# Moving the weight rings' slots in SBUF from 32 past a multiple of 64 bytes to a multiple of 64

## The chip, the cores and the metric

The kernel runs on one core of a Trainium2 chip. The metric is the device time of one execution in microseconds (us). Before the change it is 838.55 us, the median of 3 runs (837.41 to 838.63).

## The reference

A decoder trunk of two layers on one sequence of 256 tokens with 1,024 features, all in float32. Layer 0 is an S5 state-space mixer, layer 1 an attention with forget gates; each is followed by a mixture of 32 experts of which every token uses two. Cut to what matters here, the experts:

```python
for e in range(N_EXPERTS):                       # 32
    y = (jax.nn.silu(t @ w1[e]) * (t @ w3[e])) @ w2[e]   # w1, w3: 1024 x 256, w2: 256 x 1024
    out = out + gates[:, e:e + 1] * y
```

and around them

```python
h = h + gate * s5_mixer(modulate(rmsnorm(h), shift, scale))      # layer 0
h = h + gate * hier_moe(modulate(rmsnorm(h), shift, scale))
k, v, fcum = shared_kv(h)
h = h + gate * fox_mixer(modulate(rmsnorm(h), shift, scale))     # layer 1
h = h + gate * hier_moe(modulate(rmsnorm(h), shift, scale))
```

Each expert layer has 32 x 3 x 1 MB of weights. No weight is used twice, so every byte of them is read once from HBM: 297 MB in all, among them the matrices that make shift, scale and gate.

## The kernel before, in words

**Blocks and slots.** All large weights are laid out in HBM as blocks of 128 rows of 8,192 bytes (1 MB, [128, 2048] float32), one row for each SBUF partition. One DMA on SyncE's queue fetches a block into a slot, a tile named w (line 67, function fetch). The slots form a ring: new_slot (line 60) hands out the next one, and a block's DMA waits until the slot's last reader is through.

```python
 46  wpool = ctx.enter_context(tc.tile_pool(name="ring", bufs=ring))      # ring = 12
 65  def fetch(src):
 66      t = new_slot()
 67      nc.sync.dma_start(t, src)
 85      pool = es.enter_context(tc.tile_pool(name=name, bufs=n, side=side))   # in grow
```

**Rings that grow.** The 12 slots of the pool "ring" are always there. Where other tiles have been given back, grow (line 83) adds pools of slots: "ring2" (4 slots, line 337, from the experts of layer 0 on), "ring3" (5 slots, line 1072, during the experts of layer 0), "ring4" (3 slots, line 1364) and "ring5" (4 slots, line 1469) for the experts of layer 1. So layer 0's experts cycle through 21 slots, 5 of ring3 and then 16 others, and layer 1's through 19. ring3 is the only one on the right side of SBUF.

**Two sides.** Pools are placed one after the other, from the bottom of SBUF upwards (side left) or from its top downwards (side right), every tile at the next multiple of 32 bytes in its partition. On the left lie first the constants (pool "const": cols, line 96; h, line 98; and others), then the pool "small", then "ring", and above it what a stage needs. On the right are the tiles of the gating (uT, vg, uH, uL), ring3, the expert tiles P, Pr, a, aT, y, and most of the attention's tiles (xs, hn, oT, sgT, v, ws).

**The expert layers** (function moe, line 332 on). The experts go in 8 quads of 4. For a quad, gather (line 461, matmuls of line 470) collects up to 32 tokens for each of the four experts; first (line 499, matmuls of line 506) multiplies them by 8 blocks wa, the matrices w1 and w3; after silu and a transposition second (line 515, matmuls of line 521) multiplies by 4 blocks wb, the matrix w2; scatter (line 526, matmuls of line 528) adds the result to the tokens. load (line 326) issues the blocks ahead, in the order in which they are used (wa 8, wb 4, quad by quad), as far as slots are free. SyncE's queue is in order; it has 8 blocks under way and issues the next when one has landed.

**Other stages.** Before layer 0's experts runs the S5 loop (lines 796 to 1000), whose operations on VectorE (lines 840 to 951) work on tiles such as m1, m2 and cz above the ring. Between the two expert layers lie the shared keys and values and the attention (lines 1078 to 1470); there ScalarE and VectorE split each weight into two parts (lines 1125, 1126 into ws) and TensorE multiplies them (lines 1200, 1387, 1424).

Of the kernel before, what the change touches and what calls it, by code (L numbers as in the profile page):

```python
# [10 lines left out]
F32 = mybir.dt.float32  # L11
# [10 lines left out]
KD = 8  # L22
NE = 32
CAP = 32
NQ = NE // 4
EPS = 1e-6
BIG = 1e30
# [11 lines left out]
def trunk(ctx: ExitStack, tc: tile.TileContext, A, out, ring=12, ring2=4, ring3=5, ring4=3, ring5=4, lpb=2, TK=2):  # L39
# [3 lines left out]

    const = ctx.enter_context(tc.tile_pool(name="const", bufs=1))
    small = ctx.enter_context(tc.tile_pool(name="small", bufs=2))
    wpool = ctx.enter_context(tc.tile_pool(name="ring", bufs=ring))
    slots = [wpool] * ring
    turn_ = [0]
# [60 lines left out]
    V.memset(ones, 1.0)  # L109
    slot = const.tile([128, CAP], F32, name="slot")  # L110
    G.iota(slot, pattern=[[1, CAP]], base=1, channel_multiplier=0, allow_small_or_imprecise_dtypes=True)
    desc = const.tile([128, NE], F32, name="desc")
# [50 lines left out]
    def ada_cols_pe(name, j, put):  # L163

        ps = mm_tile()
        for b, w in enumerate([block(name, j, b) for b in range(4)]):
            for kk in range(2):
                for q in range(4):
                    PE.matmul(ps[32 * q:32 * q + 32, 0:256], sc32(2 * b + kk),
                              bands(w[:, 1024 * kk:1024 * kk + 1024])[:, q],  # L170
                              start=b + kk == 0, stop=b == 3 and kk == 1)
        put(ps)
        yield

    def ada_gate_pe(name, j, li, gbc, at_once=False):

        ps = mm_tile() if at_once else acc_tile()
        rows = small.tile([128, 512], F32, tag="rows", name="rows", bufs=1)
        G.memset(rows, 0.0)
        for n in range(2):  # L180
            nc.sync.dma_start(rows[32 * n:32 * n + 1, :], A["gbias"][li, n:n + 1, :])
        for b, w in enumerate([block(name, j, b) for b in range(4)]):
            for q in range(4):
                PE.matmul(ps[32 * q:32 * q + 32, :], sc32(2 * b + q // 2), w[:, 512 * q:512 * q + 512],
                          start=b == 0, stop=b == 3)
            if not at_once:
                yield
        ins = V.tensor_tensor(rows, ps, rows, op=OP.add)
        if not at_once:
            tc.keep_in_program_order(ins)  # L190
        yield
        for n in range(2):
            pt = mm_tile()
            PE.matmul(pt, pick[:, n:n + 1].to_broadcast([128, 128]), rows, start=True, stop=True)
            S.activation(gbc[:, 512 * n:512 * n + 512], pt, AF.Copy)
# [25 lines left out]
    def as_shift(bias, sh):  # L221
        return lambda ps: as_columns(ps, 8, sh, cols[:, bias:bias + 8])

    def as_gain(bias, lng, g):
        def put(ps):
            as_columns(ps, 8, g, cols[:, bias + 8:bias + 16])
            V.scalar_tensor_tensor(g, g, 1.0, cols[:, lng:lng + 8], op0=OP.add, op1=OP.mult)
        return put
# [80 lines left out]
    def router(l, sh, g):  # L309
# [12 lines left out]

    orders = [[(n, (l, q, j)) for q in range(NQ) for n, m in (("wa", 8), ("wb", 4)) for j in range(m)]
              for l in range(2)]
# [7 lines left out]
    def moe(l, sh, g, gbc, c36, slots_):  # L332
# [34 lines left out]
        def t2(n, w):  # L367
            return ma.tile([128, 2, w], F32, name=n)
# [78 lines left out]
        scs, xgs, Ps, acc = {}, {}, {}, []  # L447
        shp = [128, 4, CAP]

        def place(q):  # L450

            P = mb[0].tile([128, 2, 4, CAP], F32, tag="P", name="P", bufs=1)
            Pr = mb[0].tile([128, 2, 4, CAP], F32, tag="Pr", name="Pr", bufs=1)
            e = slice(4 * q, 4 * q + 4)
# [71 lines left out]
        def scatter(q, y, n, done=None):  # L526
            for i in range(2):
                PE.matmul(acc[i][n], scs[q][:, 128 * i:128 * i + 128], y[:, 512 * n:512 * n + 512],  # L528
                          start=q == 0, stop=q == NQ - 1, skip_group_check=True)
                if done:  # L530
                    done(i, n, acc[i][n])

        def overflow(rv):

            with tc.If(rv > CAP):
                gov = t2("gov", NE)
# [14 lines left out]
                gnext = t2("gnext", NE)  # L551
                with tc.For_i(0, NQ, 1) as q, tc.For_i(0, 2048, 512) as c:

# [61 lines left out]
        def experts(mosti, fill, done, tail=()):  # L615
            y = None
            for q in range(NQ):
                last = q == NQ - 1
                work = {}
                if q == NQ - 2:  # L620
                    scatter(q - 1, y, 1)
# [187 lines left out]
    for m in range(2):  # L809
# [5 lines left out]
    side = [ada_gate_pe("ada00g", 0, 0, gb00, True),  # L815
            ada_cols_pe("ada01", 0, as_shift(C_ADAB + 16, sh01)),
            ada_cols_pe("ada01", 1, as_gain(C_ADAB + 16, C_LNG + 8, g01)),
            ada_cols_pe("kvada", 0, as_shift(C_ADAB + 64, shkv)),
            ada_cols_pe("kvada", 1, as_gain(C_ADAB + 64, C_KVG, gkv))]
# [794 lines left out]
```

## Time and profile before

| | |
|---|---|
| median of 3 runs | 838.55 us (837.41 to 838.63) |
| the profiled execution | 838.87 us |
| its span, first to last instruction | 837.1 us |
| mean granted clock of TensorE | 0.932 |
| TensorE busy (matmuls) | 710.3 us, 85% |
| VectorE busy | 412.0 us, 49% |
| ScalarE busy | 218.8 us, 26% |
| DMA moved | 299.28 MB, mean 358 GB/s |
| of it the queue of the weights (q1) | 297.14 MB, 87.5% of 16 engines' span |

The span is what the trace covers; the time of an execution is 1.8 us more. A share of the DMA is the mean over the core's 16 DMA engines; each of them carries out rows (packets) one after the other, so that one may begin a little before the other's end and a full share reads 1.01. A block's time to landing runs from its issue on SyncE until all 128 rows are in.

### The profile page before, as it was taken

What the parts mean: (1) busy time and instruction counts of PE and PEld (TensorE: products, weight loads), DVE (VectorE), ACT (ScalarE), POOL (GpSimd) and SP (SyncE); (2) the same over time, 40 slices, a digit from 0 to 9 for tenths busy, and PEclk for the clock granted to TensorE, in tenths of its full rate; (3) what the DMA queues carried; (4) which work ended last, traced back from release to release, by engine and by line L of the source; (5) the groups of instructions that cost most, each with busy time, mean ns of one, the idle gap of its engine ahead of it and who ended that gap; (6) DMA issues with size and microseconds to landing.
All of it is one profiled execution on the core that took longest, in us unless ns stands there. A gap on an engine that the chain in (4) does not pass through costs nothing. (4 is left out here: it accounts for less than half of the span.)

```text
span 837.1 us, 13449 instructions
## 1 busy us (share of the span) xinstructions
PE 710.3 (85%) x5396; PEld 407.1 (49%) x5396; DVE 412.0 (49%) x1068; ACT 218.8 (26%) x498; POOL 51.8 (6%) x52
## 2 busy tenths in 40 slices
PE   3897999897899987676799988599998999887776
PEld 0674776584343333131286776488764333331311
DVE  7685999864422221120376589967654222221202
ACT  4332333252211110010234355456522111100100
POOL 2000000000000000000002106900000000000000
PEclk9998999998999999898769999789999999997887
DMA  9998956778999999999999996323879999999996
GB/s 370 418 417 346 385 175 254 302 300 324 418 419 420 419 418 420 420 417 416 421 418 377 412 380 230 128 104 105 350 313 404 418 420 419 419 420 419 417 413 251
DMA packets 41827, 299.28 MB, mean 358 GB/s; under 512 B 4632, under 2 KB 4760, under 8 KB 5664
## 3 DMA queue, kind: packets, MB, share of 16 engines
q1 hardware_dynamic: 41344, 297.14, 87.5%
q10 hardware_dynamic: 416, 1.23, 0.4%
q8 instruction: 44, 0.72, 0.3%
q14 instruction: 23, 0.19, 0.1%
HBM read 297.31 MB, written 1.05 MB: 356 GB/s over the span
## 5 line engine op out<-in xcount | busy, mean ns | idle before, releaser
L506 PE MATMUL mm<-w,xg 128*32 128x512 f32 x1024 | 144.3, 645 | 28.7 <-DMA w<-wa 10.9
L506 PEld LDWEIGHTS mm<-w,xg 128*32 128x32 f32 x1024 | 29.8, 112 | 118.2 <-issue 68.1
L478 ACT ACTIVATE xg<-mm,sh,g 128x128 f32<-128x128 f32 x64 | 29.3, 458 | 189.0 <-PE mm L470 172.8
L521 PE MATMUL mm<-w,aT 128*32 128x512 f32 x512 | 68.0, 647 | 12.5 <-DMA w<-wb 6.9
L1200 PE MATMUL acc<-ws,hn 128*128 128x512 f32 x288 | 74.2, 416 | 2.3 <-ACT hn L1164 2.3
L1126 DVE TENSOR_TENSOR ws<-w,ws 128x512 fp32r<-128x512 f32 x80 | 60.9, 765 | 29.6 <-ACT ws L1125 29.3
L470 PE MATMUL mm<-Pr,h 128*128 128x128 f32 x512 | 64.2, 279 | 11.2 <-DVE Pr L458 11.2
L470 PEld LDWEIGHTS mm<-Pr,h 128*128 128x128 f32 x512 | 59.8, 192 | 26.0 <-issue 18.6
L528 PE MATMUL acc<-y,Sc 128*128 128x512 f32 x128 | 65.8, 638 | 6.5 <-DVE y L524 6.5
L1125 ACT ACTIVATE ws<-w 128x512 fp32r<-128x512 f32 x80 | 50.1, 629 | 71.3 <-PE acc L1200 45.9
L1200 PEld LDWEIGHTS acc<-ws,hn 128*128 128x128 f32 x288 | 56.4, 199 | 18.1 <-ACT hn L1164 2.5
L476 DVE TENSOR_SCALAR xg<-mm,g,sh 128x128 f32<-128x128 f32 x64 | 26.2, 410 | 73.1 <-ACT xg L478 73.1
L524 DVE TENSOR_TENSOR y<-mm,gbc 128x512 f32<-128x512 f32 x32 | 22.1, 692 | 68.9 <-PE mm L521 68.6
L489 DVE COPY Sc<-mm 128x256 f32<-128x256 f32 x16 | 6.8, 425 | 86.6 <-PE mm L487 86.6
L511 ACT ACTIVATE a<-mm 128x256 f32<-128x256 f32 x16 | 6.1, 384 | 161.9 <-PE mm L506 161.9
L528 PEld LDWEIGHTS acc<-y,Sc 128*128 128x128 f32 x128 | 22.7, 198 | 47.0 <-issue 29.8
L512 DVE TENSOR_TENSOR a<-a,mm 128x256 f32<-128x256 f32 x16 | 6.7, 420 | 77.5 <-ACT a L511 77.5
L521 PEld LDWEIGHTS mm<-w,aT 128*32 128x32 f32 x512 | 14.1, 113 | 53.0 <-issue 37.1
L981 PE MATMUL acc<-w,uT 128*128 128x512 f32 x64 | 31.9, 645 | 5.7 <-ACT uT L970 5.7
L805 PE MATMUL mm<-hnT,w 128*64 128x128 f32 x512 | 32.4, 286 | 2.7 <-ACT hnT L275 2.7
L805 PEld LDWEIGHTS mm<-hnT,w 128*64 128x64 f32 x512 | 30.7, 140 | 4.4 <-ACT hnT L275 3.7
L1387 PE MATMUL acc<-hn,ws 128*128 128x256 f32 x192 | 28.5, 303 | 2.6 <-DVE ws L1126 2.6
(334 smaller groups left out, 980.9 us busy)
## 6 DMA issues: line engine op xcount, KB each, us to landing
w<-wa SPq DMA_DIRECT2D x128, 1024.0 KB, 19.9
w<-wb SPq DMA_DIRECT2D x64, 1024.0 KB, 19.9
w<-ada SPq DMA_DIRECT2D x36, 1024.0 KB, 10.6
w<-ada00s SPq DMA_DIRECT2D x8, 1024.0 KB, 18.0
w<-kvada SPq DMA_DIRECT2D x8, 1024.0 KB, 9.8
w<-win SPq DMA_DIRECT2D x4, 1024.0 KB
w<-ada00g SPq DMA_DIRECT2D x4, 1024.0 KB, 19.0
w<-woutv SPq DMA_DIRECT2D x4, 1024.0 KB, 17.6
```

Source lines behind the costliest of these rows:

```text
L470: PE.matmul(px[:, 128 * c4:128 * c4 + 128], h[:, i, 128 * c:128 * c + 128], Pr[:, i].rearrange("p a b -> p (a b)"), start=i == 0, stop=i == 1)
L476: V.tensor_scalar(xg[:, c], src, g[:, c:c + 1], sh[:, c:c + 1], op0=OP.mult, op1=OP.add)
L478: S.activation(xg[:, c], src, AF.Identity, bias=sh[:, c:c + 1], scale=g[:, c:c + 1])
L506: PE.matmul(ph[32 * s:32 * s + 32, :], xg[:, k, 32 * s:32 * s + 32], w[:, 512 * s:512 * s + 512], start=k == 0, stop=k == KD - 1)
L521: PE.matmul(py[32 * s:32 * s + 32, :], aT[:, 128 * f + 32 * s:128 * f + 32 * s + 32], w[:, 512 * s:512 * s + 512], start=f == 0, stop=f == 1)
L528: PE.matmul(acc[i][n], scs[q][:, 128 * i:128 * i + 128], y[:, 512 * n:512 * n + 512], start=q == 0, stop=q == NQ - 1, skip_group_check=True)
L805: PE.matmul(ps[64 * v:64 * v + 64, 128 * hh:128 * hh + 128], w[:, k, c0:c0 + 64], hnT[:, k, v::2], start=k == 0 and hh == 0, stop=k == KD ...
L981: PE.matmul(val[t][n], uT[:, m, 128 * t:128 * t + 128], wval[m // 2][:, c0:c0 + 512], start=m == 0, stop=m == 7)
L1125: S.activation(o[:, 0], w, AF.Copy)
L1126: V.tensor_tensor(o[:, 1], w, o[:, 0].bitcast(F32), op=OP.subtract)
L1200: PE.matmul(pk[i], src[:, k, a, 128 * i:128 * i + 128], w[:, b], start=k + a + b == 0, stop=k == KD - 1 and b == 1)
L1387: PE.matmul(po[:, 256 * m2:256 * m2 + 256], w[:, bb, kk, 128 * m2:128 * m2 + 128], hq[:, k, a, :], start=k + a + bb + m2 == 0, stop=k == K ...
```

## The change

Two tiles that nothing reads or writes are placed, one on each side: 224 bytes per partition on the left after the pool "small" and ahead of "ring", and 32 bytes on the right, at the very top.

```diff
@@ -22,6 +22,7 @@
 KD = 8
 NE = 32
 CAP = 32
+PAD_LEFT, PAD_RIGHT = 56, 8
 NQ = NE // 4
@@ -43,6 +44,9 @@
     const = ctx.enter_context(tc.tile_pool(name="const", bufs=1))
     small = ctx.enter_context(tc.tile_pool(name="small", bufs=2))
+
+    for i, (sd, n) in enumerate((("left", PAD_LEFT), ("right", PAD_RIGHT))):
+        ctx.enter_context(tc.tile_pool(name=f"pad{i}", bufs=1, side=sd)).tile([128, n], F32, name=f"pad{i}")
     wpool = ctx.enter_context(tc.tile_pool(name="ring", bufs=ring))
```

Everything placed later moves: on the left 224 bytes up, on the right 32 bytes down. Each address then changes its remainder by 64 from 32 to 0 or from 0 to 32; what lies ahead of the pads stays. The addresses in a partition, in bytes:

| tile | before | remainder by 64 (by 256) | after | remainder by 64 (by 256) |
|---|---|---|---|---|
| cols, rows of 1,424 bytes | 1,152 | 0 (128) | 1,152 | 0 (128) |
| h, rows of 4,096 bytes | 2,592 | 32 (32) | 2,592 | 32 (32) |
| slots of "ring", 12 | 23,328 + 8,192 k | 32 (32) | 23,552 + 8,192 k | 0 (0) |
| slots of ring2, ring4, ring5 | 121,632 or more | 32 (32) | 121,856 or more | 0 (0) |
| slots of ring3, 5 | 188,384 + 8,192 k | 32 (224) | 188,352 + 8,192 k | 0 (192) |
| cosT, sinT | 147,872 and 156,064 | 32 | 148,096 and 156,288 | 0 |
| m1, m2, cz (S5 loop) | 187,840 and others | 0 | 188,064 and others | 32 |
| uH, uL, vg, first ws | 184,288 and others | 32 | 184,256 and others | 0 |
| attention's ws | 217,056 and others | 32 | 217,024 and others | 0 |
| xs, hn, oT, sgT, xf, v | 184,256 and others | 0 | 184,224 and others | 32 |
| P, Pr, a, aT, y (experts) | 167,904 and others | 32 | 167,872 and others | 0 |

The program built from it has the same instructions on every engine and queue, in the same order and with the same waits; only addresses differ.

## Rows read from the trace of the kernel before

**Rows 1.** Windows: stretch; PE, PEld, DVE, ACT, POOL busy us (count); clock; DMA share; GB/s.
```profile
208.00:406.00 198.00, 162.44 (x1074) 61.81 (x1073) 43.80 (x123) 19.46 (x42) 0.22 (x2) 0.95 1.01 419
636.00:828.00 192.00, 160.18 (x1014) 60.06 (x1015) 40.81 (x110) 16.90 (x38) 0.00 (x0) 0.91 1.00 415
```

**Rows 2.** Waits of SyncE's queue, 205 to 415 us: us in total, times, longest.
```profile
SPq L67 <- DMA w<-wa: 91.8, 44, 3.5
SPq L67 <- DMA w<-wb: 53.9, 26, 2.1
...
SPq L67 <- PE mm L506: 6.8, 12, 3.4
```

**Rows 3.** Timeline of TensorE, last quad of layer 0: start, length, [idle time before].
```profile
388.00 1.06 PE L506 MATMUL mm<-w,xg 128*32 128x512 f32 x8 [1.32 <-SPq L535]
390.49 1.06 PE L506 MATMUL mm<-w,xg 128*32 128x512 f32 x8 [1.43 <-SPq L535]
...
395.48 1.93 PE L506 MATMUL mm<-w,xg 128*32 128x512 f32 x8 [0.57 <-SPq L535]
```

**Rows 4.** Chain of waits, its longest link: start, length in us.
```profile
811.28 7.34 DMA w<-wa
```

**Rows 5.** Windows: sum over 100 to 160 us, the S5 loop.
```profile
sum 60.00, PE 57.30 PEld 38.67 DVE 58.12 ACT 18.23 POOL 0.00; mean PE 19.10 PEld 12.89 DVE 19.37 ACT 6.08 POOL 0.00
```

**Rows 6.** DMA, 208 to 406 us: queue, packets, MB, share; issues, us to landing.
```profile
GB/s 407 424 424 415 420 419 422 417 414 422 424 422 417 415 422 419 417 417 422 417 422 419 420 419 419 414 422 422 424 412 417 415 424 420 409 422 424 420 401 422
...
q1 hardware_dynamic: 11353, 82.67, 100.8%
...
w<-wa SPq DMA_DIRECT2D x48, 1024.0 KB, 19.9
```

**Rows 7.** DMA, 636 to 827 us.
```profile
q1 hardware_dynamic: 10908, 79.40, 100.3%
```

**Rows 8.** DMA, 166.4 to 168.6 us: 2.2 us in which the weights come unhurried.
```profile
DMA packets 122, 0.93 MB, mean 425 GB/s; under 512 B 8, under 2 KB 8, under 8 KB 8
...
q1 hardware_dynamic: 122, 0.93, 100.3%
```

**Rows 9.** DMA, 8 to 9 us: q10 carries rows of h.
```profile
q10 hardware_dynamic: 33, 0.14, 32.8%
```

**Rows 10.** DMA, 3.8 to 4.8 us: q10 carries rows of cols.
```profile
q10 hardware_dynamic: 40, 0.06, 15.2%
```

**Rows 11.** Windows of 12.5 us in layer 0, columns as in rows 1.
```profile
232.20:244.70 12.50, 10.96 (x70) 4.55 (x70) 2.38 (x9) 0.38 (x1) 0.00 (x0) 1.00 1.01 420
244.70:257.20 12.50, 12.50 (x86) 4.96 (x85) 3.03 (x6) 1.83 (x4) 0.00 (x0) 1.00 1.01 417
...
297.40:309.90 12.50, 11.54 (x93) 5.65 (x91) 3.25 (x11) 2.21 (x5) 0.00 (x0) 1.00 1.01 417
284.90:297.40 12.50, 10.98 (x77) 3.67 (x77) 3.48 (x8) 1.30 (x3) 0.00 (x0) 1.00 1.01 419
```

**Rows 12.** Groups by line and shape, whole run: xcount | busy us, mean ns of one.
```profile
L1030 ACT ACTIVATE ws<-w 128x512 fp32r<-128x512 f32 x16 | 9.9, 628 | 6.7 <-PE mm L1053 4.5 <-DVE ws L1031 2.2
...
L1164 ACT ACTIVATE hn<-xf 128x512 fp32r<-128x512 f32 x8 | 4.8, 624 | 1.3 <-DVE xf L1160 1.2
...
L1031 DVE TENSOR_TENSOR ws<-w,ws 128x512 fp32r<-128x512 f32 x16 | 10.8, 688 | 4.0 <-ACT ws L1030 3.9
L951 DVE TENSOR_TENSOR m<-m,cosT 128x1024 f32<-128x1024 f32 x8 | 9.8, 1224 | 0.2
...
L1165 DVE TENSOR_TENSOR hn<-xf,hn 128x512 fp32r<-128x512 f32 x8 | 5.3, 690 | 0.6 <-ACT hn L1164 0.5
...
L719 DVE TENSOR_TENSOR sinT<-sinT,cosT 128x1024 f32<-128x1024 f32 x2 | 2.4, 1218 | 0.0
...
L1424 PE MATMUL acc<-ws,oT 128*128 128x512 f32 x96 | 25.0, 406 | 0.0
...
L1053 PE MATMUL mm<-ws,uH 128*128 128x512 f32 x64 | 20.8, 404 | 0.2 <-DVE ws L1031 0.2
```

## The prediction

> **What bounds the kernel now.** I read the windows first, since the page's busy shares mix stages. In two long stretches, 208 to 406 us and 636 to 828 us, the DMA engines are busy all the time (shares 1.01 and 1.00) and move 419 and 415 GB/s, while TensorE is busy for 162.4 of 198 and 160.2 of 192 us [rows 1]. These are the expert layers. The waits of SyncE's queue confirm who sets the pace there: of the 210 us from 205 to 415, the queue spends 91.8 + 53.9 = 145.7 us waiting for earlier weight blocks to land, and 6.8 us for TensorE to free a slot [rows 2]. The timeline of TensorE shows the same from the other side: in the last quad of layer 0 its groups of eight matmuls start at 388.00, 390.49, 392.98 and 395.48 us, so one block of 1 MB every 7.48 / 3 = 2.49 us, with up to 1.43 us of idle time before each group [rows 3]. The program ends the same way: the chain of waits begins with 7.34 us of a weight transfer [rows 4]. So in 390 of the 837.1 us the rate at which rows of 8,192 bytes are written into the ring slots is the time of the kernel. Elsewhere it isn't: in the S5 loop, from 100 to 160 us, VectorE is busy for 58.1 of 60 us [rows 5].
>
> **What the change does to that.** It issues nothing new. Every engine and queue keeps its instructions, their order and their waits; no DMA is added, split or moved. Only addresses move: ring slots go from 32 past a multiple of 64 to a multiple of 64. The whole question is therefore the price of a write, read or row at one offset against the other, at three kinds of places.
>
> **Term 1, the weight rows in the two stretches.** How many: queue q1 carries 82.67 MB in 198 us and 79.40 MB in 191 us [rows 6, 7]. Together 162.07 MB are 154.6 blocks of 1.0486 MB, or 19,784 rows of 8,192 bytes, 1,236 for each of the 16 DMA engines. One nanosecond per row is so worth 1.24 us of the kernel.
>
> What a row costs now: in a quiet window of 2.2 us, 122 packets on q1, 8 of them signals under 512 bytes, take 100.3% of 16 engines, which is 35.3 us, or 309 ns for each of the 114 rows (the signals are under 0.1 us in all) [rows 8]. The rows of h (4,096 bytes, also 32 past a multiple of 64) take 32.8% of 16 us for 33 packets: 159.0 ns [rows 9]. Two points give a line: 150 ns for 4,096 bytes, 0.0366 ns per byte, with 9.0 ns fixed per row.
>
> What an aligned row costs: the trace has one transfer with a destination that already is a multiple of 64, the table cols at byte 1,152, with rows of 1,424 bytes. Its 40 packets from 3.8 to 4.8 us take 15.2% of 16 us, 60.8 ns each [rows 10]. The line through the unaligned rows gives 0.0366 × 1,424 + 9.0 = 61.1 ns. The aligned row is 0.3 ns below it, within the rounding of the shares. I take 0.3 ns, because it is the only row in this trace at the new offset: 0.3 × 1.24 = **0.4 us saved**. The bounds: nothing at one end (61.1 and 60.8 are then the same), and at the other the whole fixed part of 9.0 ns, if alignment were all that it is made of: 11.1 us. A loss is not excluded by principle, but an aligned row has no more bytes than an unaligned one, and cols shows none.
>
> The nearest check on a finer address than 64 is inside this kernel. The right-hand ring has slots at 224 past a multiple of 256, the left-hand slots lie at 32 past it, and one round of the ring takes five blocks into the right and sixteen into the left. By count of blocks the right-hand ones fill 244.7 to 257.2 and 297.4 to 309.9 us: 417 and 417 GB/s, against 420 and 419 in the left-hand stretches just ahead [rows 11]. That is 0.6% for 192 bytes of offset, so for the 32 bytes of this change a sixth, 0.1% of 389 us, again 0.4 us.
>
> A rule of the Trainium skill speaks on just this. DMA: Bandwidth & Descriptors, section "How a descriptor splits into AXI transactions", says that a transaction must start at a multiple of 256 bytes, so that a row with another start pays for bytes that it doesn't use. By it a row would cost 257 beats of 32 bytes in a left-hand slot now and 263 in a right-hand one, 2.3% more; the windows show 0.6%, so the trace agrees in sign and not in size. By the rule the change takes one beat off each row.
>
> **Term 2, the engines' operands.** TensorE reads the slots, ScalarE and VectorE split them, and many tiles trade offsets (some lose the multiple of 64: those of the S5 loop, and hn, oT, xs in the attention part). Same work at both offsets is in the trace. ScalarE's copy of 512 columns takes 628 ns from and to tiles 32 off a multiple of 64, and 624 ns between aligned ones; VectorE's subtraction of 512 columns takes 688 ns 32 off and 690 ns aligned; with 1,024 columns 1,218 ns 32 off and 1,224 ns where the result is aligned; TensorE's 512-column matmul has a mean of 404 ns with uH (32 off) and 406 ns with oT (aligned) as weights [rows 12]. The differences between 32 off and aligned are -6 to +4 ns, of both signs. I take **0**. In the two stretches even 4 ns would be hidden behind the 1.43 us of idle time per block [rows 3].
>
> **Term 3, everything else.** The pads take 256 bytes of each partition and no instruction writes them: 0.
>
> **Sum.** The profiled execution took 838.87 us, span 837.1 and 1.8 around it; its 0.4 us less is 838.5. The median of the three runs is 838.55, 0.3 below the profiled one, and the prediction is for a median: 838.55 - 0.4 = **838.2 us**. What a measurement of this kernel can tell from no change is about 0.2%, 1.7 us, so this is "the same".
>
> **Rivals.**
> 1. *One piece less per row.* The write of a row is cut at some coarser grid, and the slots' start off that grid costs one more 32-byte piece. Price: 32 × 0.0366 = 1.17 ns per row, 1.45 us in all, 837.1 us. For: the right-hand slots are slower by 0.6%. Against: cols shows 0.3 and not 1.2 ns. It stays just under 1.7 us, so mostly "the same". The skill's section named above is this case.
> 2. *The offset costs only under load.* A row takes 309 ns when the queue is quiet; but in the two stretches a block takes 389 / 154.6 = 2.516 us, where 8 rows and a signal would take 8 × 309 + 9 = 2.481 us. Over 154.6 blocks that is 5.4 us of waiting which no quiet row shows. If writes that straddle 64 bytes are what waits (two neighbouring rows' pieces meeting in one place, say), most of it goes: 838.55 - 5.4 = 833.1 us. For: the loss exists, and the trace has no aligned transfer under full load. Against: it comes in part as single gaps, the rate of the forty slices between 208 and 406 us lies between 401 and 424 GB/s [rows 6], which looks like something that happens now and then and not to every row. If it and the fixed 9.0 ns both went, the time would be 822; nothing supports that.
> 3. *Slower: the S5 loop loses its alignment.* The tiles m1, m2, cz and their like go from a multiple of 64 to 32 past one, in the stretch from 100 to 160 us where VectorE is busy for 58.1 of 60 us [rows 5]. If VectorE's operations there grew by 5%, the kernel would take 2.9 us longer, 841.4. It decides from 1.7 / 58 = 2.9%, some 36 ns on a 1,224 ns operation. Against: 1,218 ns with both operands 32 off [rows 12].
> The change can't fail to do what it says: the addresses are fixed when the program is built.
>
> **How the numbers follow.** Forecast (0 to 1 us saved) 0.50, rival 1 0.14, rival 2 in whole or in part 0.27, rival 3 0.09. Rival 1 lies so near the limit that I give 0.04 of it to "faster". Faster by over 0.2%: 0.27 + 0.04 = 0.31. Within: 0.50 + 0.10 = 0.60. Slower: 0.09. The range reaches down to 832.0, so that all of rival 2 and 1.1 us of run to run differences are in it (the runs differ by 1.2 us), and up to 839.8, which leaves out rival 3 and half the tail above the median: about 0.15 outside. The forecast's own range is 837.3 to 839.2.
>
> **What would show it right or wrong.** Right: in the profile after, the windows of the two stretches again give 419 and 415 GB/s within 1, a block of layer 0's last quad every 2.49 us, 19.9 us from issue to landing [rows 6]. Rival 1 shows as 0.4% more: 2.48 us per block, 421 GB/s. Rival 2 as a rate of 422 GB/s or more and a landing of 19.6 us. Rival 3 as longer means of VectorE's lines 918 to 951 with the two stretches unchanged in length. I am wrong if the rate of the loaded stretches moves by over 1%, either way: then the cost of an offset under load is not that of a quiet row, and the step from cols to the weights is the one that failed.

## The result, and the profile after

The change brings **830.09 us** (median of 4 runs, 827.79 to 830.81) against 838.59 us (median of 4 runs of the kernel before, 837.41 to 840.59). The ratio is 0.9891, with a 95% interval from 0.9863 to 0.992: faster by 1.1%, where I had forecast 0.4 us and no difference that can be measured. The profiled execution took 830.81 us with a span of 829.0, where it was 838.87 and 837.1 before; the mean granted clock of TensorE is 0.938 (0.932 before).

The windows of the two expert layers come first, since the forecast hung on their rate. The columns are those of rows 1.

```profile
208.00:403.00 195.00, 162.42 (x1070) 61.66 (x1070) 43.65 (x123) 19.29 (x41) 0.22 (x2) 0.95 1.01 425
632.00:819.00 187.00, 156.87 (x1012) 59.84 (x1012) 40.49 (x110) 16.70 (x37) 0.00 (x0) 0.93 1.01 424
```

The DMA engines are as full as before (1.01), and move 425 and 424 GB/s where they moved 419 and 415 [rows 1]. TensorE has the same work in it (162.42 us against 162.44 in the first). The view of the DMA for the first of these windows gives the GB/s of forty slices, the queue of the weights and a block's time from issue to landing, as rows 6 do:

```profile
GB/s 418 429 429 420 429 427 427 423 425 427 430 422 425 430 427 423 423 430 427 422 425 425 430 427 425 425 429 425 427 429 418 418 429 429 425 425 427 427 410 429
...
q1 hardware_dynamic: 11367, 82.78, 100.8%
...
w<-wa SPq DMA_DIRECT2D x48, 1024.0 KB, 19.6
```

The queue carries 82.78 MB in 195 us, where it took 198 us for 82.67 [rows 6]. The slices have moved as a whole: from 401 to 424 they went to 410 to 430, so it isn't that a few gaps were closed. A block lands after 19.6 us (19.9 before).

The timeline of TensorE in the last quad of layer 0, as in rows 3:

```profile
385.75 1.06 PE L510 MATMUL mm<-w,xg 128*32 128x512 f32 x8 [1.26 <-SPq L539]
388.18 1.94 PE L510 MATMUL mm<-w,xg 128*32 128x512 f32 x8 [1.36 <-SPq L539]
...
393.04 1.89 PE L510 MATMUL mm<-w,xg 128*32 128x512 f32 x8 [0.50 <-SPq L539]
```

(The change adds four lines, so L506 is now L510 and L67 is L71.) Three blocks in 7.29 us are one in 2.43 us, against 2.49 [rows 3]. Still TensorE waits for each of these blocks, and the waits of SyncE's queue, 205 to 412 us, say the same as rows 2:

```profile
SPq L71 <- DMA w<-wa: 92.1, 46, 3.1
SPq L71 <- DMA w<-wb: 53.7, 27, 2.2
...
SPq L71 <- PE mm L510: 4.6, 10, 2.1
```

So the bound is what it was, weight rows on their way into the ring. It is the row that has become cheaper.

**Where the 8.1 us of the spans went.** The starts of the weight rows in the trace date each of the 282 blocks (from 0) of a profiled execution. Blocks 58 to 141 and 206 to 281 are those of the expert layers that wait for little but the DMA. Beside the pair stand means over two groups of kernels, one execution of each: before with the experiments e1, e2 and e4 below, whose left-hand slots are off a multiple of 256, and after with e3 and e6, whose left-hand slots are on one.

```
us                                      before   after   before, e1, e2, e4   after, e3, e6
start of the span to block 58           194.0    194.9   194.2                194.4
block 58 to 141, layer 0's last         209.0    205.7   208.6                205.7
block 141 to 206, in layer 1            232.4    230.1   230.5                229.7
block 206 to 281, the last              188.2    185.1   188.0                185.1
block 281 to the end                     13.6     13.2    13.5                 13.1
```

The two stretches of the expert layers give 3.3 and 3.1 us in the pair, 2.8 and 2.9 in the means. The kernel's first weight stream gets shorter too (the 24 blocks from block 3 to block 27 in 60.2 us, 61.4 before), but the S5 loop behind it takes what it took, and block 58 comes no sooner. The stretch between the layers differs by 2.3 us in the pair and 0.9 in the means, and by up to 3.2 us within the first group, so I count nothing there.

### The profile page after: what moved, and what is told of

It is laid out like the page before. It is cut to its first block, busy times and chain, and to the rows that moved or that the text cites. A ratio compares the mean times of both kernels' runs of the same rounds, so it can differ in the third digit from the quotient of the medians.

```text
span 829.0 us, 13449 instructions
## 1 busy us (share of the span) xinstructions
PE 707.3 (85%) x5396; PEld 409.8 (49%) x5396; DVE 411.8 (50%) x1068; ACT 218.7 (26%) x498; POOL 51.9 (6%) x52
## 5 line engine op out<-in xcount | busy, mean ns | idle before, releaser
L510 PE MATMUL mm<-w,xg 128*32 128x512 f32 x1024 | 141.7, 636 | 27.1 <-DMA w<-wa 11.8
L510 PEld LDWEIGHTS mm<-w,xg 128*32 128x32 f32 x1024 | 29.8, 112 | 115.8 <-issue 68.4
L532 PE MATMUL acc<-y,Sc 128*128 128x512 f32 x128 | 64.0, 623 | 7.0 <-DVE y L528 7.0
## 6 DMA issues: line engine op xcount, KB each, us to landing
w<-wb SPq DMA_DIRECT2D x64, 1024.0 KB, 19.6
```

The source lines that it names most:

```text
L510: PE.matmul(ph[32 * s:32 * s + 32, :], xg[:, k, 32 * s:32 * s + 32], w[:, 512 * s:512 * s + 512], start=k == 0, stop=k == KD - 1)
```

## The experiments

Open were: which pad does it, which remainder counts (64, as the slots' new place suggests, or something coarser), whether it is the DMA or an engine's operands, whether the read or the write, and why the quiet rows of the prediction showed nothing. The first five keep the kernel whole and only change the pads; the last four are nothing but a stream of blocks. Each stream is a single execution, and its stages are compared with one another.

**e1_both32: every ring slot on a multiple of 64, none on one of 256.**

```diff
-PAD_LEFT, PAD_RIGHT = 56, 8
+PAD_LEFT, PAD_RIGHT = 8, 8
```

> Pads of 32 and 32 bytes: left-hand slots at 64 past a multiple of 256, right-hand ones at 192 past, all at multiples of 64. Theory A (a row costs more under load when its slot starts off a multiple of 64, whatever the coarser remainder): a block every 2.453 us in the expert layers as with the change, time 830 us, within 2 of the changed kernel. Theory B (the grid is 256 bytes; only slots at its multiples gained): the left-hand slots are off the grid again, a block every 2.49 us, 838 us. A grid of 128 gives the same as B here, since 64 is no multiple of it.

Measured: 836.56 us (12 runs, 834.68 to 837.64), before 838.23 (29 runs); ratio 0.9972 (0.9957 to 0.9987). Every tile has the remainder by 64 that the change gives it, and some three quarters of the gain are gone. (An offset of 64 is slightly cheaper than one of 32, in the stream m1_stream below by 6 of 39 ns per block; for 155 blocks that is about 1 us. Where the rest of what is left comes from is not shown.) So neither the multiple of 64 nor what the change does to the engines' operands by 64 is the cause.

**e2_both64: the remainders by 64 of before, other remainders by 256** (left-hand slots 96 past a multiple of 256, right-hand ones 160).

```diff
-PAD_LEFT, PAD_RIGHT = 56, 8
+PAD_LEFT, PAD_RIGHT = 16, 16
```

> Pads of 64 and 64 bytes: everything moves as in the change, by other amounts, but every remainder by 64 stays that of the kernel before (slots at 32). Theory A: a block every 2.493 us, 838.6 us, no difference from the kernel before. Theory C (any move gains, for instance because left-hand and right-hand tiles lie at other distances from each other or other rows of HBM and SBUF meet): about 830 us.

Measured: 836.45 us (12 runs, 833.39 to 840.15); ratio 0.9986 (0.997 to 1.0002). 64 past and 96 past are alike, and near before's 32 past.

**e3_left and e4_right: one pad alone.**

```diff
-    for i, (sd, n) in enumerate((("left", PAD_LEFT), ("right", PAD_RIGHT))):
+    for i, (sd, n) in enumerate((("left", PAD_LEFT),)):
```

> The left pad of 224 bytes alone. Right-hand slots stay at 32 past a multiple of 64; they take 21 of the some 155 blocks of the two DMA-bound stretches. Theory A: the gain of the change less 21/155 of its stream part of 6.2 us, so 831 us. If the right-hand tiles of the engines were what gained (theory C'): 838 us.

> The right pad of 32 bytes alone. Theory A: only the 21 right-hand blocks gain 0.04 us each, 0.8 us, so 837.7 us, at the limit of what can be told from no change. Theory C' (the right-hand tiles of the engines are what gained): 831 us.

Measured: the left pad alone 830.03 us (6 runs, 828.3 to 833.79), ratio 0.9904 (0.988 to 0.9928); the right pad alone 837.94 us (12 runs), ratio 1.0 (0.998 to 1.002). The 224 bytes on the left are the whole change.

**e6_both256: the right-hand ring on a multiple of 256 too.**

```diff
-PAD_LEFT, PAD_RIGHT = 56, 8
+PAD_LEFT, PAD_RIGHT = 56, 56
```

> Pads of 224 and 224 bytes: the right-hand ring too lies at multiples of 256. By theory B the 21 right-hand blocks can gain at most 0.04 us each, 0.8 us; as they come in runs of five and the stream without computation kept its full pace for the first four blocks after the start moved off the grid, about 0.1 us of it is left: 830 us, the same as the changed kernel.

Measured: 830.06 us (6 runs, 828.11 to 832.91), before 838.29 (11 runs); ratio 0.9908 (0.9887 to 0.993). Nothing more than e3, whose right-hand slots lie 224 past. The same stretch of layer 0, 220 to 400 us, in the windows of before, e1_both32, e4_right, then of e3_left, e6_both256 and the change:

```profile
220.00:400.00 180.00, 149.07 (x980) 57.76 (x980) 37.54 (x103) 15.30 (x35) 0.15 (x2) 0.95 1.01 419
```

```profile
220.00:400.00 180.00, 152.14 (x983) 58.99 (x981) 38.26 (x105) 15.72 (x35) 0.00 (x0) 0.93 1.01 420
```

```profile
220.00:400.00 180.00, 150.26 (x984) 58.53 (x982) 38.25 (x105) 16.15 (x36) 0.00 (x0) 0.94 1.01 419
```

```profile
220.00:400.00 180.00, 152.00 (x998) 58.69 (x998) 38.41 (x105) 15.48 (x35) 0.22 (x2) 0.93 1.01 425
```

```profile
220.00:400.00 180.00, 152.91 (x996) 59.41 (x998) 39.06 (x107) 16.08 (x36) 0.22 (x2) 0.93 1.01 426
```

```profile
220.00:400.00 180.00, 150.98 (x990) 58.35 (x990) 38.02 (x103) 15.51 (x35) 0.22 (x2) 0.95 1.01 426
```

The last column has two levels, 419 to 420 and 425 to 426, and the left-hand slots' remainder by 256 (32, 64, 32 against three times 0) is what goes with them; the clock, in the third column from the end, does not.

**m1_stream: the rate against the offset, without any engine.** One DMA per block into 12 slots that start at multiples of 256, in stages of 36 blocks, each stage with its own offset.

```diff
+OFFSETS = (0, 32, 64, 96, 128, 16, 4, 0)
...
+    for off in OFFSETS:
+        for _ in range(ROUNDS):
+            for w in ws:
...
+                nc.sync.dma_start(w[:, off // 4:off // 4 + 2048], A[name][tuple(at)])
```

> No computation at all: 288 weight blocks of 1 MB streamed into 12 slots that nothing reads, in eight stages of 36 blocks whose rows start at 0, 32, 64, 96, 128, 16, 4 and again 0 bytes past a multiple of 256; the output is x unchanged. Theory A with the cost in the DMA writes themselves: 2.453 us per block (427 GB/s) in the stages at 0, 64, 128 and 0, and 2.493 us (420 GB/s) or more at 32, 96, 16 and 4. Theory D (the cost is a meeting of DMA writes with the engines' reads of SBUF, since quiet rows didn't show it): no difference between the stages, 2.453 us in all of them, as no engine reads. Theory B (grid of 256): only the stages at 0 are at 2.453 us.

Measured, by windows inside the stages at 32, 64, 96, 128, 16, 4 and again 0 bytes (columns: busy time of VectorE and GpSimd, clock, DMA share, GB/s):

```profile
100.00:180.00 80.00, 0.00 (x0) 0.00 (x0) 1.00 1.01 421
190.00:270.00 80.00, 0.00 (x0) 0.00 (x0) 1.00 1.01 422
280.00:360.00 80.00, 0.00 (x0) 0.00 (x0) 1.00 1.01 422
368.00:448.00 80.00, 0.00 (x0) 0.00 (x0) 1.00 1.01 422
458.00:538.00 80.00, 0.00 (x0) 0.00 (x0) 1.00 1.01 419
548.00:628.00 80.00, 0.00 (x0) 0.00 (x0) 1.00 1.01 419
640.00:700.00 60.00, 0.00 (x0) 0.00 (x0) 1.00 1.01 428
```

No engine runs, and the two levels of the kernel are there. Any offset from 4 to 128 bytes costs about the same. By the starts of the rows in the trace a block takes 2,453 ns (median) at 0, in the first and in the last stage, and 2,492, 2,486, 2,484, 2,483, 2,501 and 2,501 ns at 32, 64, 96, 128, 16 and 4 (which row of a block is taken moves these by up to 3 ns). In rows, of which each DMA engine has 8 per block, 39 ns are 4.9 ns for a row 32 bytes past. The slots lie in turn at remainders 0 and 256 by 512, so 256 suffices.

The same trace answers why quiet rows showed no cost. Windows of four blocks each, the last four at 0 and the first eight at 32:

```profile
86.10:95.90 9.80, 0.00 (x0) 0.00 (x0) 1.00 1.01 427
95.90:105.70 9.80, 0.00 (x0) 0.00 (x0) 1.00 1.01 428
105.70:115.50 9.80, 0.00 (x0) 0.00 (x0) 1.00 1.01 420
```

The first four blocks off the grid still run at full rate. The cost comes with the fifth.

**m2_source: the read's side or the write's.** The same stream, each stage with a start in HBM and one in SBUF (bytes past a multiple of 256). The edits of this and the next two experiments are shown against m1_stream, with only the lines that matter.

```diff
-OFFSETS = (0, 32, 64, 96, 128, 16, 4, 0)
+STAGES = ((0, 0), (32, 0), (128, 0), (32, 32), (128, 128), (0, 192), (0, 224), (0, 0))
...
-                nc.sync.dma_start(w[:, off // 4:off // 4 + 2048], A[name][tuple(at)])
+                o = 262144 * (n % 127) + src // 4
+                nc.sync.dma_start(w[:, off // 4:off // 4 + 2048],
+                                  flat[o:o + 262144].rearrange("(p n) -> p n", n=2048))
```

> Again a stream of 288 blocks without computation, eight stages of 36; now the start in HBM is moved too. (Start of the source past a multiple of 256 bytes, start in the slot): (0, 0), (32, 0), (128, 0), (32, 32), (128, 128), (0, 192), (0, 224), (0, 0); the output is x unchanged. Theory W (only where the write starts counts, on a grid of 256): 2.453 us per block at (0, 0), (32, 0), (128, 0) and (0, 0), 2.48 to 2.50 in the other four. Theory R (the read pays as well): (32, 0) and (128, 0) are slow too. Theory D (what counts is whether source and destination are at the same remainder): (32, 32) and (128, 128) at 2.453, (32, 0) and (128, 0) slow.

Measured, by windows in the stages (32, 0), (128, 0), (32, 32) and (0, 224):

```profile
110.00:180.00 70.00, 0.00 (x0) 0.00 (x0) 1.00 1.01 428
195.00:270.00 75.00, 0.00 (x0) 0.00 (x0) 1.00 1.01 427
285.00:360.00 75.00, 0.00 (x0) 0.00 (x0) 1.00 1.01 421
...
555.00:630.00 75.00, 0.00 (x0) 0.00 (x0) 1.00 1.01 421
```

A start in HBM that is 32 or 128 off costs nothing; only the place in SBUF counts. Offsets of 192 and 224 (2,485 and 2,492 ns per block) cost no more than 128 and 32.

**m3_rows: per row or per byte.** The block in one, two or four DMAs, with rows of 8,192, 4,096 and 2,048 bytes, each at 0 and at 32 (the code counts a row in elements of 4 bytes).

```diff
+STAGES = ((2048, 0), (2048, 32), (1024, 0), (1024, 32), (512, 0), (512, 32), (2048, 0))
...
+                for c in range(0, 2048, row):
+                    nc.sync.dma_start(w[:, off // 4 + c:off // 4 + c + row], A[name][tuple(at)][:, c:c + row])
```

> A stream of 252 blocks without computation, seven stages of 36, each block fetched by 1, 2 or 4 DMAs: rows of 8,192 bytes at slot starts 0 and 32 past a multiple of 256, rows of 4,096 at 0 and 32, of 2,048 at 0 and 32, and again 8,192 at 0; the output is x unchanged. If the price is one per row (one more piece, 39 ns / 8 = 4.9 ns): 32 costs 0.04 us per block with 8,192, 0.08 with 4,096 and 0.16 with 2,048 over the stage at 0 before it. If it is one per byte (every 256 bytes of the row are cut in two): 0.04 us per block in all three.

Measured, medians of the time per block: 2,453 to 2,492 ns at 8,192 bytes, 2,497 to 2,560 at 4,096, 2,583 to 2,710 at 2,048. With 8, 16 and 32 rows per block and DMA engine, that is 4.9, 3.9 and 4.0 ns per row: the price hangs on the row and not on its bytes. The mean rates agree for 4,096 bytes and don't settle 2,048. The windows of the stages 4,096 at 0 and at 32, then 2,048 at 0 and at 32:

```profile
195.00:270.00 75.00, 0.00 (x0) 0.00 (x0) 1.00 1.03 420
290.00:360.00 70.00, 0.00 (x0) 0.00 (x0) 1.00 1.03 410
395.00:460.00 65.00, 0.00 (x0) 0.00 (x0) 1.00 1.03 377
470.00:560.00 90.00, 0.00 (x0) 0.00 (x0) 1.00 1.05 384
```

In the third there are pauses between blocks that the medians leave out, so for 2,048 bytes the price is read from undisturbed blocks alone.

**m4_mixed: how many blocks off the grid are free.** The stream with destinations that take turns in a fixed pattern, stages of 48 blocks.

```diff
+STAGES = ((0, 1), (1, 2), (3, 4), (3, 6), (9, 12), (1, 1), (0, 1))
...
+            for i, w in enumerate(ws):
+                off = 32 if i % period < shifted else 0
```

> All computation is left out: again only the stream of 1 MB blocks through 12 slots (x is copied to the output), in seven stages of 48 blocks, now with destinations that take turns between a multiple of 256 and 32 past one: none off, 1 of 2, 3 of 4, 3 of 6 (in a row), 9 of 12 (in a row), all off, none off. Open is why quiet rows and the right-hand ring, whose five blocks come between sixteen others, showed no cost. Theory A, the cost starts only after three to four blocks in a row off the grid, and a block on it ends that: 2,453 ns per block in 1 of 2, 3 of 4 and 3 of 6, some 2,470 in 9 of 12 (five or six of twelve pay), 2,492 in all off; so 428, 428, 428, 425 and 421 GB/s. Rival B, every row off the grid costs the same whatever comes before it and only a first start is delayed: 2,473, 2,483, 2,473, 2,483 and 2,492 ns, so 424, 422, 424, 422 and 421 GB/s. Rival C, a debt that blocks on the grid pay off only slowly: 1 of 2 and 3 of 6 at full pace, 3 of 4 and 9 of 12 near 2,480 and alike.

Measured, by windows in the stages 1 of 2, 3 of 4, 3 of 6, 9 of 12, all, none:

```profile
150.00:233.00 83.00, 0.00 (x0) 0.00 (x0) 1.00 1.01 426
270.00:350.00 80.00, 0.00 (x0) 0.00 (x0) 1.00 1.01 423
390.00:470.00 80.00, 0.00 (x0) 0.00 (x0) 1.00 1.01 426
510.00:590.00 80.00, 0.00 (x0) 0.00 (x0) 1.00 1.01 423
630.00:710.00 80.00, 0.00 (x0) 0.00 (x0) 1.00 1.01 420
750.00:825.00 75.00, 0.00 (x0) 0.00 (x0) 1.00 1.01 427
```

By the starts of the rows, in steady state:

```
pattern                     1 of 2   3 of 4   3 of 6   9 of 12   all     none
ns per block, mean          2,462    2,478    2,462    2,478     2,493   2,453
above none                  9        25       9        25        40      0
(off - on / 2) / all x 40   10       25       10       25        40      0
```

Neither of the first two theories holds. The length of a run does not decide (1 of 2 and 3 of 6 are alike, 3 of 4 and 9 of 12 too), and the cost is not proportional to the blocks off the grid (half of them cost a quarter). It is nearest to the third, a debt that blocks on the grid pay off, except that it pays off less than I had assumed: one block on the grid makes good for half a block off it (last line of the table). In the pattern 9 of 12 the nine blocks take 2,453, 2,457, 2,492, 2,499, 2,493, 2,492, 2,492, 2,498 and 2,493 ns, so after three on the grid two run free; after the 36 of m1_stream it was four, so there is an upper limit. What in the chip keeps this account is not shown.

## Why the prediction was wrong

**What bounds the kernel, and where one nanosecond per row counts: right.** The gain that can be located lies in the weight rows of the two expert layers, and 1.24 us per ns is confirmed: a row costs 4.9 ns less, 4.9 × 1.24 = 6.1 us, and the two stretches of the expert layers became 5.7 to 6.3 us shorter. The measured gain is 8.5 us, with an interval from 6.7 to 11.5; e3_left and e6_both256 give 8.0 and 7.7, with intervals that begin at 6.0 and 5.9. The 6 us are accounted for; whether the other 2 are gained between the two layers or are differences between runs stays open.

**Term 1, the step from cols to the weights: it failed,** as the prediction had named for a rate that moves by over 1% (it moved from 419 to 425 and from 415 to 424). It took 0.3 ns per row where the stream pays 4.9. Two things were wrong in it, and both could be seen.
- *It compared rows off the grid with rows off the grid.* cols lies 128 past a multiple of 256 [rows 10], h 32 past [rows 9], the right-hand slots 224 and the left-hand ones 32 past [rows 11]; m1_stream and m2_source show that all these pay about the same. No row of data in the kernel before begins at a multiple of 256, so none could show what such a row costs. The table of addresses has a column by 256 in which this stands. The sixth part that I took of the right-hand ring's 0.6% assumed a price that grows with the offset, and it doesn't. Nor is the 0.6% a price at all: by the starts of the rows the right-hand blocks 78 to 82 and 99 to 103 took 2,505 and 2,507 ns each, the sixteen left-hand ones between them 2,509, so the trace did not agree even in sign with the beats that I had counted.
- *It took rested rows for loaded ones.* The 309 ns of rows 8 are the price on the grid. In a full stream a row off it takes 313 to 320 ns most of the time, and 309 mainly after a rest (in the steady part of m1_stream's stage at 32 bytes, 7% of the rows did). In the trace of before 10,210 of 36,096 weight rows took 309 ns, after the change 34,577. The window of rows 8 isn't a quiet one, as its share of 100.3% says. It lies behind gaps in the stream, where the debt has been paid, and around it the kernel before runs off the grid at full rate:

```profile
164.50:172.00 7.50, 7.50 (x33) 5.98 (x32) 6.88 (x15) 3.46 (x8) 0.00 (x0) 1.00 1.01 427
```

The same holds of the rows of h: their 159 ns is what rows of 4,096 bytes take on the grid in m3_rows. The loaded price stood in rows 6: 100.8% of 16 engines over 198 us, for 10,092 rows of 8,192 bytes, is 316 ns a row with its share of the signals, and 311 in the same view after.

**Rival 2, the offset costs only under load: right that load is needed, near in size by luck, wrong in cause.** Of the rivals its estimate of 5.4 us was the nearest, and its signs came (422 GB/s or more, landing after 19.6 us). But the 5.4 us are 2.516 us per block less 2.481, and neither is the rate of one kind of block: an undisturbed block takes 2.493 us off the grid and 2.453 on it. The 2.516 holds some 0.02 us of other waiting, which the change leaves (2.470 us per block after, in the first window), and the 2.481 lies 0.03 above what a block takes on the grid; the two errors nearly cancel. Its mechanism, pieces that straddle 64 bytes, is refuted by e1_both32, where no slot does and the rate is 420. The pads work because 224 bytes bring the left-hand slots to a multiple of 256.

**Rival 1, a piece less per row on a coarser grid: right on the grid, wrong in size.** The grid is coarser, as it said; that one more piece is what costs is not shown, and the rows off the grid that run free after a rest speak against it. It priced the piece at 1.17 ns by its bytes, a quarter of the 4.9 measured, and the price is no matter of bytes: 4 and 16 bytes past (2,501 ns per block) cost more than 128 past (2,483). The section "How a descriptor splits into AXI transactions" of DMA: Bandwidth & Descriptors in the Trainium skill names the multiple of 256, and for the writes into SBUF every run agrees. It counts a surplus of beats that grows with the offset and tells it of what is read; here the price is nearly the same from 32 to 224 bytes, and a read's start in HBM 32 or 128 past costs nothing (428 and 427 GB/s).

**Term 2, the engines' operands: right.** The groups of lines after, beside rows 12:

```profile
L1034 ACT ACTIVATE ws<-w 128x512 fp32r<-128x512 f32 x16 | 9.9, 627 | 6.9 <-DVE ws L1035 3.6 <-PE mm L1057 3.3
...
L955 DVE TENSOR_TENSOR m<-m,cosT 128x1024 f32<-128x1024 f32 x8 | 9.8, 1223 | 0.2
...
L1057 PE MATMUL mm<-ws,uH 128*128 128x512 f32 x64 | 20.8, 404 | 0.2 <-DVE ws L1035 0.2
```

They were 628, 1,224 and 404 ns, with the other remainder by 64. Term 3 stands as well: the right-hand pad alone changes nothing (e4_right, ratio 1.0). **Rival 3** falls with Term 2: the tiles of the S5 loop went 32 past a multiple of 64, and VectorE is busy for 57.70 us of the 60 from 100 to 160 us, where it was 58.12 [rows 5].

```profile
sum 60.00, PE 57.30 PEld 38.67 DVE 57.70 ACT 18.00 POOL 0.00; mean PE 57.30 PEld 38.67 DVE 57.70 ACT 18.00 POOL 0.00
```

**The range** began at 832.0, 1.9 us above the result, because I took rival 2 for the outermost case. The bound that Term 1 itself had worked out, 11.1 us for the whole fixed part of a row, was not excluded by any row on the grid, and should have weighed more.

## What to carry to other kernels

Where a kernel is bound by DMA rows into SBUF, look at each destination's address in its partition by 256 bytes, and pad once so that the ring's slots begin at a multiple of it: here 224 bytes per partition and no instruction gave 1%. Price it per row of a full stream, and measure it with a bare stream of the same rows, since single rows and rows after a rest show nothing. The five right-hand slots, a small part of a round of 21, gained nothing that can be measured when they were moved as well.

## What the runs showed of the hardware that I had not expected

- A row written to SBUF from a start that is not a multiple of 256 bytes costs 3.9 to 4.9 ns more in a full stream (rows of 2,048 to 8,192 bytes, 32 bytes past), and at 8,192 bytes 3.8 to 6.0 ns for any of the offsets 4, 16, 32, 64, 96, 128, 192 and 224. A start of the read in HBM 32 or 128 past a multiple of 256 was free.
- The cost is not paid row by row. After 36 blocks on the grid the first four off it ran at 428 GB/s and the next four at 420; in mixtures one block on the grid made good for half a block off it. So in the changed kernel four of the five right-hand blocks, 192 past, run at nearly full pace behind sixteen on the grid: in one of their runs 99, 95, 95, 93 and 42% of the rows took 309 ns.
